# A gated short convolution moved from transposed tiles to token rows

## The chip, the cores and the metric

The kernel runs on one core of a Trainium2 chip. Its time is the device time in microseconds (us), median over the timed runs; 259.68 us before the change (three runs, 259.32 to 259.75). The engines of the core are TensorE (PE, with PEld for its weight loads), VectorE (DVE), ScalarE (ACT), GpSimd (POOL) and SyncE (SP), which here issues every transfer.

## The reference

Two layers over 256 tokens of width 1024, in float32. Layer 0 is a gated short convolution, layer 1 attention over one block of 256 keys. The part that the change touches:

```
b_gate, c_gate, xv, z = split(rms_norm(x) @ w_in, 4)     # 256 x 1024 each
u = c_gate * xv
conv[t] = w[0] * u[t-2] + w[1] * u[t-1] + w[2] * u[t]     # per channel, zero before token 0
y = b_gate * conv * silu(z)
h = x + y @ w_out
```

## The kernel before, in words

**Products.** Every dense product is done in three float32r products on PE: high part by high part, high by low, low by high. A weight unit is 256 rows by 512 columns of a matrix; there are 80 of them. A load pair brings two units (1 MB, line 314, tile `raw`, a ring of four); ACT rounds a unit into `whi` (line 355), DVE subtracts to get `wlo` (line 362), both in rings of five units; PE then runs 12 products of 512 columns (lines 419 to 421). Counting from 0, units 0 to 3 come with x in the first loads (`in_first`), and pair n (n from 2) holds units 2n and 2n+1.

**The convolution layer.** Its input projection runs in two halves of 512 channels: units 0 to 15 and 16 to 31. Each half has four blocks of four units, in the order C, x, z, B. A block fills two PSUM banks (tile `mm`), one for each 128 tokens, with tokens on the partitions and channels along the free dimension. Before the change C is scaled out of PSUM (`scaled`, line 477) and multiplied with x to u (`times`, line 485). Then PE turns u (`transposed`, line 451: eight 128x128 transposes for a half, `at<-ident,row`), so that channels lie on the partitions and tokens along the free dimension. There a shift by one or two tokens is an offset in the access, and a tap is one number for each partition: ACT scales by the last tap (line 512), DVE adds the other two (line 520). B times silu(z) is turned as well (eight more transposes), multiplied with the convolution (line 539) and split into `ys` (lines 493 and 497), the left-hand operand of the output projection, units 32 to 39. So a half has two pieces of eight transposes: u's, one unit after the x block (units 9 and 25 follow them), and y's, one unit after the B block (units 17 and 33 follow them).

**What sets the order.** All work is listed as operations with an engine, an estimated duration, what they read and write and which ring buffer they take. A planner (`Plan`) places them by these estimates, twelve times over with priorities from the round before, and keeps the best; the engines then run their instructions in that fixed order. SP's transfers are in it too: a transfer that waits holds up every later one on SP, and an operation that waits holds up all later ones of its engine.

Of the kernel before, what the change touches and what calls it, by code (L numbers as in the profile page):

```python
# [8 lines left out]
F32 = mybir.dt.float32  # L9
# [5 lines left out]
P = 128  # L15
# [15 lines left out]
)  # L31
NU = len(UNITS)
WARM = 8
NSM = 48

# [167 lines left out]
def hybrid_kernel(  # L203
    ctx: ExitStack,
    tc: tile.TileContext,
    first: bass.AP,
    xt: bass.AP,
    w: bass.AP,
    out: bass.AP,
# [40 lines left out]

    act.preload_act_table(AF.Silu)

    sm = one.tile([P, NSM], F32, name="sm")
# [8 lines left out]
    kk2 = one.tile([P, 2, 4, 2, S], F32R, name="kk2")  # L262
    kT, klz = kk2[:, :, :, 0], kk2[:, :, :, 1]
    qT = one.tile([P, 2, 4, S], F32R, name="qT")
    vv = one.tile([P, 2, 4, 4, HD], F32R, name="vv")
    g0, g1, taps = sm[:, 0:8], sm[:, 8:16], sm[:, 16:40]
# [52 lines left out]
    load_first(0, "w")  # L319
    for k in range(1, KT):  # L320
        load_first(k)
    op("DVE", 80, lambda: dve.tensor_copy(sm, piece(0, -NSM, 0)), r=[(firsts[0], (0, "x"))], w=["sm"])
# [14 lines left out]

    op("POOL", 900, lambda: make_identity(nc, ident), w=["ident"])
    op("POOL", 1000, distances, w=["dist"])
    for s in range(2):  # L340
        r2 = slice(HD - s * HD, P - s * HD)
        op("POOL", 950, lambda s=s, r2=r2: pool.memset(klz[r2, s].bitcast(F32), 0.0), w=[("klz0", s)])


    his, los = [whi_t() for _ in range(NU)], [wlo_t() for _ in range(NU)]
# [142 lines left out]
        )  # L488
        return o

    def split_y(y, j0, nj):
        js = range(j0, j0 + nj)
        op("ACT", 150 + 250 * nj, lambda: act.copy(ys[:, j0 : j0 + nj, 0], y()[:, 0:nj]), r=[y], w=[("ys", j, 0) for j in js])
        op(
            "DVE",
            180 + 280 * nj,
            lambda: dve.tensor_sub(ys[:, j0 : j0 + nj, 1], y()[:, 0:nj], ys[:, j0 : j0 + nj, 0].bitcast(F32)),
            r=[y] + [("ys", j, 0) for j in js],
            w=[("ys", j, 1) for j in js],
        )  # L500

    def conv(hf, i, us_):
        j0 = 4 * hf + 2 * i
        bank = transposed(lambda t: us_[t](), us_, [2 * i * P, (2 * i + 1) * P])
        c = bias_t()
        for jj in range(2):
            j = j0 + jj
            b = lambda jj=jj: bank()[:, jj * S : (jj + 1) * S]
            op(
                "ACT",  # L510
                440,
                lambda b=b, j=j, jj=jj: act.activation(c()[:, jj], b(), AF.Copy, scale=taps[:, 16 + j : 17 + j]),
                r=[bank, "sm"],
                w=[(c, jj)],
            )
            for d in (1, 2):
                op(
                    "DVE",
                    460,
                    lambda b=b, j=j, jj=jj, d=d: dve.scalar_tensor_tensor(  # L520
                        c()[:, jj, d:S],
                        b()[:, 0 : S - d],
                        taps[:, 8 * (2 - d) + j : 8 * (2 - d) + j + 1],
                        c()[:, jj, d:S],
                        op0=ALU.mult,
                        op1=ALU.add,
                    ),
                    r=[bank, "sm"],
                    w=[(c, jj)],
                )  # L530
        return c

    def gated(hf, i, c, qs):
        bank = transposed(lambda t: qs[t](), qs, [2 * i * P, (2 * i + 1) * P])
        y = y_t()
        op(
            "DVE",
            700,
            lambda: dve.tensor_mul(y(), c(), bank().rearrange("p (j s) -> p j s", s=S)),
            r=[(c, 0), (c, 1), bank],  # L540
            w=[y],
        )
        split_y(y, 4 * hf + 2 * i, 2)

    for hf in range(2):
        banks = block(xs, "xs")
        if hf == 0:
            stats0()
        cs = [scaled(banks[t], t) for t in range(2)]
        banks = block(xs, "xs")  # L550
        us_ = [times(banks[t], t, cs[t]) for t in range(2)]
        convs = [conv(hf, i, us_) for i in range(2)]
        banks = block(xs, "xs")
        sl = [scaled(banks[t], t, AF.Silu) for t in range(2)]
        banks = block(xs, "xs")
        qs = [times(banks[t], t, sl[t]) for t in range(2)]
        for i in range(2):
            gated(hf, i, convs[i], qs)


    for cb in range(2):
# [50 lines left out]

    def small_ones():
        dve.tensor_scalar(epsv, v1, EPS, None, op0=ALU.mult)
        dve.tensor_mul(gg, sm[:, 40:41], sm[:, 41:42])
# [11 lines left out]
    def queries_or_keys(name, bank, t):  # L627
        sq, ss, n = row_t(), ss_t(), row_t()
        op("ACT", 620, lambda: act.activation(sq(), bank(), AF.Square), r=[bank], w=[sq])

        op("DVE", 680, lambda: dve.tensor_reduce(ss()[:, 0:8], sq().rearrange("p (h d) -> p h d", d=HD), axis=AX.X, op=ALU.add), r=[sq], w=[ss])

        def inverse():
            pool.tensor_scalar(ss()[:, 0:8], ss()[:, 0:8], 1.0 / HD, epsv[:, t : t + 1], op0=ALU.mult, op1=ALU.add)
            pool.tensor_tensor(ss()[:, 8:16], ss()[:, 0:8], nhalf, op=ALU.pow)  # L635

        op("POOL", 1900, inverse, r=["nhalf", "epsv"], w=[ss])
        op(
            "DVE",
            700,  # L640
            lambda: dve.tensor_mul(
                n().rearrange("p (h d) -> p h d", d=HD),
                bank().rearrange("p (h d) -> p h d", d=HD),
                ss()[:, 8:16, None].to_broadcast([P, 8, HD]),
            ),
            r=[bank, ss],
            w=[n],
        )
        tb = at_t()

        def turn():
            for i in range(4):
                pe.transpose(tb()[:, i * P : (i + 1) * P], n()[:, i * P : (i + 1) * P], ident)  # L653

        op("PE", 440, turn, r=[n, "ident"], w=[tb])
        ts = slice(t * P, (t + 1) * P)
        psv = lambda: tb().rearrange("p (j t) -> p j t", t=P)
        for s in range(2):
            r, r2 = slice(s * HD, s * HD + HD), slice(HD - s * HD, P - s * HD)
            if name == "k":  # L660
                hi = kT[r, s, :, ts]
                op("ACT", 680, lambda r=r, hi=hi: act.activation(hi, psv()[r], AF.Copy, scale=gg[r]), r=[tb, "gg"], w=[("k", t, s, 0)])
                op(
                    "DVE",
                    745,
                    lambda r=r, s=s, hi=hi: dve.scalar_tensor_tensor(
                        klz[r, s, :, ts], psv()[r], gg[r], hi.bitcast(F32), op0=ALU.mult, op1=ALU.subtract
                    ),
                    r=[tb, "gg", ("k", t, s, 0)],
                    w=[("kl", t, s)],  # L670
                )
                op("POOL", 640, lambda r2=r2, s=s, hi=hi: pool.tensor_copy(kT[r2, s, :, ts], hi.bitcast(F32)), r=[("k", t, s, 0)], w=[("k", t, s, 1)])
            else:
                hi = qT[r, s, :, ts]
                op("ACT", 600, lambda r=r, hi=hi: act.copy(hi, psv()[r]), r=[tb], w=[("q", t, s, 0)])
                op(
                    "DVE",
                    690,
                    lambda r=r, r2=r2, s=s, hi=hi: dve.tensor_sub(qT[r2, s, :, ts], psv()[r], hi.bitcast(F32)),
                    r=[tb, ("q", t, s, 0)],  # L680
                    w=[("q", t, s, 1)],
                )

    def values(bank, t):
# [31 lines left out]
    def pair(j, s2):  # L716
# [6 lines left out]

        def scores():
            for s in range(2):
                a, b, o = qT[:, s, jj, 0:P], qT[:, s, jj, P:S], sc[s]()
                o1 = o[:, 0:S].rearrange("p (i k) -> p i k", k=P)
                pe.matmul(o1, lhsT=a, rhs=kk2[:, s, jj, :, 0:P], start=True, stop=True)
                pe.matmul(o[:, S:512], lhsT=b, rhs=kT[:, s, jj], start=True, stop=False)  # L729
                pe.matmul(o[:, S:512], lhsT=b, rhs=klz[:, s, jj], start=False, stop=True)  # L730

        op(
            "PE",
            710,
            scores,
            r=[(n, t, s, i) for n in "kq" for t in range(2) for s in range(2) for i in range(2)]
            + [("kl", t, s) for t in range(2) for s in range(2)]
            + [("klz0", s) for s in range(2)],
            w=sc,
        )  # L740
        cut = ((slice(0, P), slice(P, S)), (slice(P, 384), slice(0, S)))
# [194 lines left out]
```

## Time and profile before

| | |
|---|---|
| timed runs, median | 259.68 us (259.32 to 259.75) |
| the profiled execution, its own time | 259.06 us |
| its span | 257.3 us |
| busy: PE / DVE / ACT / POOL | 98% / 73% / 63% / 19% |
| bytes moved by the DMA engines | 45.33 MB, 176 GB/s over the span |

Times within the program are counted from the start of the span. Instructions on PE overlap, so the distance between two starts tells more than the duration of one. A mean duration can mix shapes; where it matters a stretch of the timeline is read instead.

### The profile page before, as it was taken

The page shows a single profiled execution, that of the slowest core. Times are in us where ns is not written, and L with a number is a line of the kernel's source. Part 1 is how long each engine was busy: PE and PEld are TensorE (multiplying, and loading weights), DVE is VectorE, ACT ScalarE, POOL GpSimd, SP SyncE. Part 2 cuts the span into 40 slices and gives each one's busy share as a digit, 9 for nine tenths or more (in the row PEclk, how much of TensorE's full clock was granted, in tenths as well). Part 3 has the DMA queues.
Part 4 walks back from the last instruction along what each step waited for, and adds up shares of the span by engine and source line. Part 5 has one row for each costly group of instructions (what it writes and reads, how often), then busy time and mean ns, then how long its engine had stood idle before and what let it go on. Part 6 is the DMA issues. An engine that isn't in the chain of part 4 may idle for free.

```text
span 257.3 us, 3436 instructions
## 1 busy us (share of the span) xinstructions
PE 251.8 (98%) x1198; PEld 206.8 (80%) x1198; DVE 188.7 (73%) x335; ACT 163.3 (63%) x286; POOL 49.7 (19%) x76
## 2 busy tenths in 40 slices
PE   8999999999999999999999999999999999999994
PEld 3688888888888888888888888888888888888873
DVE  2874985575558458667767976984999899977973
ACT  4868655345445535474557668996887777988720
POOL 5001000000000000000636511242164901045230
PEclk9999999999999999999999999999999999999999
DMA  6999985554666444654655454053094504400004
GB/s 216 398 395 416 383 318 164 167 171 161 225 223 201 163 163 163 176 190 173 227 169 211 138 191 163 3 169 157 3 284 152 219 3 164 164 0 3 0 0 163
DMA packets 12657, 45.33 MB, mean 176 GB/s; under 512 B 864, under 2 KB 1248, under 8 KB 12640
## 3 DMA queue, kind: packets, MB, share of 16 engines
q1 hardware_dynamic: 12640, 45.12, 49.6%
q8 instruction: 9, 0.15, 0.2%
q14 instruction: 8, 0.07, 0.1%
HBM read 44.06 MB, written 1.05 MB: 175 GB/s over the span
## 4 chain that ended last, share of the span: by engine, by line
PE 87%; DVE 4%; ACT 3%; DMA 2%; issue 1%; POOLq 0%; SPq 0%; POOL 0%
PE mm L421 26%; PE mm L419 26%; PE mm L420 26%; DMA raw<-in_first_dram 2%; PE at L451 2%; PE at L799 2%; PE at L653 1%; DVE wlo L362 1%; DVE y L838 1%; ACT whi L355 1%; PE at L820 1%; ACT prob L761 1%; DVE pp L806 1%; PE at L730 1%; PE at L729 1%
## 5 line engine op out<-in xcount | busy, mean ns | idle before, releaser
L362 DVE TENSOR_TENSOR wlo<-raw,whi 128x1024 fp32r<-128x1024 f32 (+1 forms) x84 | 98.0, 1175 | 43.0 <-ACT whi L355 42.7
L355 ACT CAST whi<-raw 128x1024 fp32r<-128x1024 f32 (+1 forms) x84 | 84.5, 1012 | 69.7 <-PE mm L421 56.5
L419 PE MATMUL mm<-whi,xs 128*128 128x512 f32 x252 | 100.3, 398 | 0.2 <-ACT xs L373 0.2
L421 PE MATMUL mm<-whi,xs 128*128 128x512 f32 x252 | 98.5, 391 | 0.0
L420 PE MATMUL mm<-wlo,xs 128*128 128x512 f32 x252 | 98.3, 390 | 0.0
L421 PEld LDWEIGHTS mm<-whi,xs 128*128 128x128 f32 x252 | 47.3, 188 | 10.4 <-DVE xs L380 0.2
L419 PEld LDWEIGHTS mm<-whi,xs 128*128 128x128 f32 x252 | 47.4, 188 | 9.4 <-ACT xs L373 0.6
L420 PEld LDWEIGHTS mm<-wlo,xs 128*128 128x128 f32 x252 | 47.4, 188 | 9.0
L419 PE MATMUL mm<-whi,ys 128*128 128x512 f32 (+1 forms) x64 | 25.4, 397 | 0.0
L421 PE MATMUL mm<-whi,ys 128*128 128x512 f32 (+1 forms) x64 | 24.9, 389 | 0.3 <-POOL ys L844 0.3
L420 PE MATMUL mm<-wlo,ys 128*128 128x512 f32 (+1 forms) x64 | 24.7, 386 | 0.0
L459 POOL TENSOR_TENSOR stat<-stat,nhalf 128x2 f32<-128x2 f32 x2 | 1.4, 709 | 118.1 <-DVE stat L458 118.1
L838 DVE TENSOR_TENSOR y<-at,y 64x256 f32<-64x256 f32 x32 | 13.5, 421 | 4.6 <-ACT y L836 3.8
L721 POOL TENSOR_SCALAR bias<-dist 128x256 f32<-128x256 f32 x16 | 9.1, 569 | 30.5 <-DVE sums L751 28.5
L761 ACT ACTIVATE prob<-neg,sums 128x256 f32<-128x256 f32 (+1 forms) x32 | 14.3, 449 | 1.0 <-DVE sums L751 0.9
L421 PEld LDWEIGHTS mm<-whi,ys 128*128 128x128 f32 x64 | 12.0, 188 | 3.2 <-POOL ys L844 0.7
L420 PEld LDWEIGHTS mm<-wlo,ys 128*128 128x128 f32 x64 | 12.1, 188 | 2.1
L419 PEld LDWEIGHTS mm<-whi,ys 128*128 128x128 f32 x64 | 12.0, 188 | 2.0
L635 POOL TENSOR_TENSOR ss<-ss,nhalf 128x8 f32<-128x8 f32 x8 | 13.1, 1641 | 0.7
L844 POOL TENSOR_TENSOR ys<-y,ys 128x256 fp32r<-128x256 f32 x8 | 7.7, 962 | 18.1 <-ACT ys L840 18.1
L775 POOL TENSOR_TENSOR sg<-row,sums 128x128 f32<-128x128 f32 x16 | 7.1, 463 | 16.9 <-ACT row L711 10.6
L802 ACT CAST pp<-at 128x384 fp32r<-128x384 f32 x16 | 7.5, 480 | 2.0 <-PE at L799 1.9
(95 smaller groups left out, 260.8 us busy)
## 6 DMA issues: line engine op xcount, KB each, us to landing
raw<-in_w_dram SPq DMA_DIRECT2D x38, 1024.0 KB, 4.9
raw<-in_first_dram SPq DMA_DIRECT2D x7, 384.0 KB, 6.5
h<-in_x_dram SPq DMA_DIRECT2D x2, 512.0 KB, 8.2
out_dram<-row SPq DMA_DIRECT2D x3, 256.0 KB, 2.5
raw<-in_first_dram SPq DMA_DIRECT2D x1, 256.0 KB, 2.7
out_dram<-row SPq DMA_DIRECT2D x2, 128.0 KB, 2.2
raw<-in_first_dram SPq DMA_DIRECT2D x1, 152.0 KB, 2.6
```

The lines of the kernel that those rows point to most:

```text
L355: lambda c=c, src=src: act.copy(his[u]()[:, c], src()),
L362: lambda c=c, src=src: dve.tensor_sub(los[u]()[:, c], src(), his[u]()[:, c].bitcast(F32)),
L419: pe.matmul(o, lhsT=a, rhs=wh, start=(k == first_k), stop=False)
L420: pe.matmul(o, lhsT=a, rhs=wl, start=False, stop=False)
L421: pe.matmul(o, lhsT=b, rhs=wh, start=False, stop=(k == KT - 1))
L635: pool.tensor_tensor(ss()[:, 8:16], ss()[:, 0:8], nhalf, op=ALU.pow)
L721: op("POOL", 450, lambda s=s, slope=slope: pool.tensor_scalar(b()[:, s], dist, slope, 1.0, op0=ALU.mult, op1=ALU.mult), r=["dist", "epsv"] ...
L761: lambda s=s, c=c, i=i, neg=neg: act.activation(p[s]()[:, c], neg()[:, c], AF.Exp, bias=sums()[:, i : i + 1], scale=-1.0, accum_out=sums() ...
L775: lambda t=t: pool.tensor_mul(sg()[:, t].rearrange("p (s d) -> p s d", d=HD), s2[t]()[:, jj * P : (jj + 1) * P].rearrange("p (s d) -> p s ...
L802: op("ACT", 480, lambda s=s, tb=tb: act.copy(pp()[:, s, 0], tb()[:, 0:384]), r=[tb], w=[(pp, (s, 0))])
L838: op("DVE", 430, lambda s=s, r=r, c=c: dve.tensor_add(y()[r, 1], av[s]()[r, c], y()[r, 1]), r=[av[s]], w=[(y, s)])
L844: lambda: pool.tensor_sub(ys[:, j, 1], y()[:, 0], ys[:, j, 0].bitcast(F32)),
```

## The change: tokens stay on the partitions

u is no longer turned. With tokens on the partitions a shift by d tokens moves rows to other partitions, so SP issues transfers within the chip: rows 0 to 127-d of u (both token halves) go to rows d to 127 of a second tile, and the last d rows of the first token half go to the head of the second. The taps, one number for each channel, now vary along the free dimension; a copy for every partition is loaded (12 KB for each partition, 1.57 MB, line 334 of the changed kernel). DVE multiplies the shifted and unshifted u by the taps and adds (five operations of 128x1024), multiplies silu(z) with the result (two of 128x512) and that with B; only this y is turned. The tiles for taps, u and shifted u share their memory with the keys and queries of the attention layer, which come later; zeroing the unused half of the keys' low parts moves behind the convolution.

```diff
-NSM = 48
+NSM = 32
...
+    kk_t = ring("kk", 1, [P, 4096], F32R, one)
+    qq_t = ring("qq", 1, [P, 2048], F32R, one)
+    early, shifted, kkb, qqb = kk_t(), qq_t(), kk_t(), qq_t()
...
     load_pair(2)
+    op("SP", us(P * 12288), lambda: sp.dma_start(early()[:, 0:3072].bitcast(F32), taps_b), w=[(early, "taps")])
...
-    def conv(hf, i, us_):
-        j0 = 4 * hf + 2 * i
-        bank = transposed(lambda t: us_[t](), us_, [2 * i * P, (2 * i + 1) * P])
-        c = bias_t()
...
+    def conv(hf, banks, cs):
+        for d in (1, 2):
+            op("POOL", 300, lambda d=d: pool.memset(u_before(d)[0:d, 0], 0.0), w=[(shifted, (d, "zero"))])
+        for t in range(2):
+            op(
+                "DVE",
+                740,
+                lambda t=t: dve.scalar_tensor_tensor(
+                    u_at(t), banks[t](), r0[:, t : t + 1], cs[t](), op0=ALU.mult, op1=ALU.mult
+                ),
+                r=[banks[t], cs[t], "r0"],
+                w=[(early, ("u", t))],
+            )
+        for d in (1, 2):
+            op(
+                "SP",
+                1400,
+                lambda d=d: sp.dma_start(u_before(d)[d:P], u_both()[0 : P - d]),
+                r=[(early, ("u", t)) for t in range(2)],
+                w=[(shifted, (d, "main"))],
+            )
+            op(
+                "SP",
+                480,
+                lambda d=d: sp.dma_start(u_before(d)[0:d, 1], u_at(0)[P - d : P]),
+                r=[(early, ("u", 0))],
+                w=[(shifted, (d, "head"))],
+            )
+        tb = lambda k: tapsb(hf, k)[:, None, :].to_broadcast([P, 2, 512])
...
+                lambda d=d: dve.tensor_mul(u_before(d), u_before(d), tb(2 - d)),
...
+        op("DVE", 1230, lambda: dve.tensor_mul(u_both(), u_both(), tb(2)), r=[(early, "taps")], w=[(early, ("u", t)) for t in range(2)])
...
+            lambda: dve.tensor_add(u_before(1), u_before(1), u_before(2)),
...
+            lambda: dve.tensor_add(u_before(1), u_before(1), u_both()),
...
+    def gated(hf, sl):
...
+                lambda t=t: dve.tensor_mul(sl[t](), sl[t](), u_before(1)[:, t]),
...
+    def output(hf, i, ys_):
+        bank = transposed(lambda t: ys_[t](), ys_, [2 * i * P, (2 * i + 1) * P])
...
+        op("ACT", 620, lambda: act.copy(ys[:, j0 : j0 + 2, 0], ps()), r=[bank], w=[("ys", j, 0) for j in js])
...
-        us_ = [times(banks[t], t, cs[t]) for t in range(2)]
-        convs = [conv(hf, i, us_) for i in range(2)]
+        conv(hf, banks, cs)
         banks = block(xs, "xs")
         sl = [scaled(banks[t], t, AF.Silu) for t in range(2)]
+        gated(hf, sl)
         banks = block(xs, "xs")
-        qs = [times(banks[t], t, sl[t]) for t in range(2)]
+        ys_ = [times(banks[t], t, sl[t]) for t in range(2)]
```

How the orders differ at three places. First SP, from the middle of the first half's loads on; before, only weight loads stand there (`raw`), each waiting for a free buffer:

```order
L314 DMA raw<-in_w_dram 128x2x1024 [waits DMAHW5_49,DVE_49]
L314 DMA raw<-in_w_dram 128x2x1024 [waits DMAHW6_49,DVE_49]
L314 DMA raw<-in_w_dram 128x2x1024 [waits DMAHW7_49,DMAHW3_49,DVE_49]
L314 DMA raw<-in_w_dram 128x2x1024 [waits DMAHW4_49,DMAHW0_49,DVE_49]
L314 DMA raw<-in_w_dram 128x2x1024 [waits DMAHW1_49,DVE_49]
```

After, the first of these rows is pair 8's load, `kk` is the tile that holds the taps and u, `qq` the one that holds the shifted u:

```order
L324 DMA raw<-in_w_dram 128x2x1024 [waits DMAHW5_49,DVE_49]
L334 DMA kk<-in_taps_dram 128x3072
L517 DMA qq<-kk 127x1024 [waits DMAHW3_49,DVE_49]
L524 DMA qq<-kk 1x16x32 [waits DMAHW4_49]
L517 DMA qq<-kk 126x1024
L524 DMA qq<-kk 2x512 [waits DMAHW6_49]
L324 DMA raw<-in_w_dram 128x2x1024 [waits DMAHW7_49,Activation_49]
L324 DMA raw<-in_w_dram 128x2x1024 [waits DMAHW0_49,DVE_49]
```

The taps and the four transfers of u stand between pair 8's load and pair 9's.

Second DVE, first half. Before, behind the product that makes u (line 485), tap products (line 520) between weight splits (line 362):

```order
L485 SCALAR_TENSOR_TENSOR row<-mm,stat,row 128x512 [waits PE_49,Pool_49]
L485 SCALAR_TENSOR_TENSOR row<-mm,stat,row 128x512 [waits PE_49]
L362 TENSOR_TENSOR wlo<-raw,whi 128x1024 [waits Activation_49]
L362 TENSOR_TENSOR wlo<-raw,whi 128x1024 [waits DMAHW7_49,Activation_49]
L362 TENSOR_TENSOR wlo<-raw,whi 128x1024 [waits Activation_49]
L520 SCALAR_TENSOR_TENSOR bias<-at,sm,bias 128x255 [waits PE_49,Activation_49]
```

After, from the split of unit 12 to the products that make y; the two rows with line 534 are the tap products of the shifted u:

```order
L370 TENSOR_TENSOR wlo<-raw,whi 128x1024 [waits DMAHW7_49,Activation_49]
L507 SCALAR_TENSOR_TENSOR kk<-mm,stat,row 128x512 [waits Pool_49]
L507 SCALAR_TENSOR_TENSOR kk<-mm,stat,row 128x512 [waits PE_49]
...
L370 TENSOR_TENSOR wlo<-raw,whi 128x1024 [waits DMAHW1_49,Activation_49]
L534 TENSOR_TENSOR qq<-qq,kk 128x1024 [waits DMAHW4_49,DMAHW3_49,DMAHW2_49]
L534 TENSOR_TENSOR qq<-qq,kk 128x1024 [waits DMAHW6_49,DMAHW5_49]
L538 TENSOR_TENSOR kk<-kk 128x1024 [waits DVE_49]
L542 TENSOR_TENSOR qq<-qq 128x1024 [waits DVE_49]
L549 TENSOR_TENSOR qq<-qq,kk 128x1024 [waits DVE_49]
L370 TENSOR_TENSOR wlo<-raw,whi 128x1024 [waits Activation_49]
L559 TENSOR_TENSOR row<-row,qq 128x512 [waits DVE_49]
L493 SCALAR_TENSOR_TENSOR row<-mm,stat,row 128x512 [waits DVE_49,PE_49] x2
```

The split ahead of line 534 is unit 16's, the one behind line 549 unit 17's; the five operations of the convolution stand in one block between them, and the first two wait for transfers.

Third DVE, second half, after the change, from the products that make u:

```order
L507 SCALAR_TENSOR_TENSOR kk<-mm,stat,row 128x512 [waits PE_49] x2
L370 TENSOR_TENSOR wlo<-raw,whi 128x1024 [waits DMAHW4_49,Activation_49]
L370 TENSOR_TENSOR wlo<-raw,whi 128x1024 [waits Activation_49]
L534 TENSOR_TENSOR qq<-qq,kk 128x1024 [waits DMAHW1_49,DMAHW0_49,Pool_49]
L370 TENSOR_TENSOR wlo<-raw,whi 128x1024 [waits DMAHW5_49,Activation_49]
L534 TENSOR_TENSOR qq<-qq,kk 128x1024 [waits DMAHW3_49,DMAHW2_49]
L370 TENSOR_TENSOR wlo<-raw,whi 128x1024 [waits Activation_49]
L538 TENSOR_TENSOR kk<-kk 128x1024 [waits DVE_49]
L370 TENSOR_TENSOR wlo<-raw,whi 128x1024 [waits DMAHW6_49,Activation_49]
L542 TENSOR_TENSOR qq<-qq 128x1024 [waits DVE_49]
L549 TENSOR_TENSOR qq<-qq,kk 128x1024 [waits DVE_49]
```

Here the splits of units 28 and 29 stand ahead of the first tap product, those of units 30, 31 and 32 behind the first, the second and the third; units 33 to 35 follow behind the gates. On PE the eight transposes of u are gone from each half, and those of y stand where the gate's stood, between units 16 and 17 and between units 32 and 33.

## Rows read from the trace of the kernel before

**Rows 1.** The page: busy time by engine, and the chain that ended last.

```profile
PE 251.8 (98%) x1198; PEld 206.8 (80%) x1198; DVE 188.7 (73%) x335; ACT 163.3 (63%) x286; POOL 49.7 (19%) x76
...
PE 87%; DVE 4%; ACT 3%; DMA 2%; issue 1%; POOLq 0%; SPq 0%; POOL 0%
```

**Rows 2.** Waits of PE: line, releaser, us in total, times, longest.

```profile
PE at L273 <- DVE nhalf L330: 1.2, 1, 1.2
PE mm L421 <- POOL ys L844: 0.3, 1, 0.3
```

**Rows 3.** The chain in order of time, 50 to 101 us: start, us, what.

```profile
53.80 0.87 PE at L451 x8
...
76.48 0.87 PE at L451 x8
...
99.17 0.87 PE at L451 x8
```

**Rows 4.** Timeline of PE around the first transposes: start, us, instruction.

```profile
30.95 1.04 PE L451 MATMUL at<-ident,row 128*128 128x128 f32 x8
31.74 0.47 PE L419 MATMUL mm<-whi,xs 128*128 128x512 f32 x1
32.05 0.39 PE L420 MATMUL mm<-wlo,xs 128*128 128x512 f32 x1
```

**Rows 5.** Timeline of PE, 0 to 16 us; the last two are 20 products apart.

```profile
1.17 3.60 PE L273 MATMUL at<-zero 128*128 128x512 bf16 x8 [1.17 <-DVE nhalf L330]
4.57 1.96 PE L405 MATMUL mm<-whi,xs 128*128 128x512 f32 x4
...
11.22 0.39 PE L419 MATMUL mm<-whi,xs 128*128 128x512 f32 x1
...
15.75 0.39 PE L421 MATMUL mm<-whi,xs 128*128 128x512 f32 x1
```

**Rows 6.** Groups by line: instruction, count, busy us, mean ns, idle before.

```profile
L520 DVE SCALAR_TENSOR_TENSOR bias<-at,sm,bias 128x255 f32<-128x255 f32 (+1 forms) x16 | 6.7, 473 | 0.0
...
L512 ACT ACTIVATE bias<-at,sm 128x256 f32<-128x256 f32 x8 | 3.1, 473 | 0.0
...
L539 DVE TENSOR_TENSOR y<-bias,at 128x512 f32<-128x512 f32 x4 | 2.7, 684 | 1.7 <-PE at L451 1.7
```

**Rows 7.** Timeline of DVE, 26 to 47 us.

```profile
27.96 1.40 DVE L485 SCALAR_TENSOR_TENSOR row<-mm,stat,row 128x512 f32<-128x512 f32 x2
29.28 2.35 DVE L362 TENSOR_TENSOR wlo<-raw,whi 128x1024 fp32r<-128x1024 f32 x2
...
41.31 1.23 DVE L362 TENSOR_TENSOR wlo<-raw,whi 128x1024 fp32r<-128x1024 f32 x1 [1.10 <-ACT whi L355]
...
46.76 1.22 DVE L362 TENSOR_TENSOR wlo<-raw,whi 128x1024 fp32r<-128x1024 f32 x1 [1.50 <-ACT whi L355]
```

**Rows 8.** Timeline of DVE, 86 to 104 us.

```profile
101.99 1.28 DVE L497 TENSOR_TENSOR ys<-y,ys 128x512 fp32r<-128x512 f32 x2
```

**Rows 9.** Stretches of PE: PE busy, granted clock, DMA share, GB/s.

```profile
10.00:12.00 2.00, 2.00 (x10) 1.00 1.04 419
26.00:28.00 2.00, 2.00 (x11) 1.00 1.03 422
```

**Rows 10.** Timeline of SP, 24 to 34 us: issues of load pairs 8 to 10.

```profile
26.93 6.92 SPq L314 DMA_DIRECT2D raw<-in_w_dram  x3
```

**Rows 11.** The page: DMA packets, and the queue that SP issues to.

```profile
DMA packets 12657, 45.33 MB, mean 176 GB/s; under 512 B 864, under 2 KB 1248, under 8 KB 12640
...
q1 hardware_dynamic: 12640, 45.12, 49.6%
```

**Rows 12.** The page: DMA issues, count, KB each, median us from issue to landing.

```profile
raw<-in_w_dram SPq DMA_DIRECT2D x38, 1024.0 KB, 4.9
...
raw<-in_first_dram SPq DMA_DIRECT2D x1, 152.0 KB, 2.6
```

More of the change, by code (lines that the diff above doesn't have):

```diff
@@ L251, in hybrid_kernel @@
     act.preload_act_table(AF.Silu)
-    sm = one.tile([P, NSM], F32, name="sm")
+    sm = one.tile([P, 48], F32, name="sm")
     ident = one.tile([P, P], F32, name="ident")
@@ L489, in times @@
         return o
-    def split_y(y, j0, nj):
-        js = range(j0, j0 + nj)
-        op("ACT", 150 + 250 * nj, lambda: act.copy(ys[:, j0 : j0 + nj, 0], y()[:, 0:nj]), r=[y], w=[("ys", j, 0) for j in js])
+    def conv(hf, banks, cs):
[27 more added lines that the diff above has]
+        tb = lambda k: tapsb(hf, k)[:, None, :].to_broadcast([P, 2, 512])
+        parts = ("zero", "main", "head")
+        for d in (1, 2):
+            op(
+                "DVE",
+                1230,
+                lambda d=d: dve.tensor_mul(u_before(d), u_before(d), tb(2 - d)),
+                r=[(early, "taps")],
+                w=[(shifted, (d, p)) for p in parts],
+            )
+        op("DVE", 1230, lambda: dve.tensor_mul(u_both(), u_both(), tb(2)), r=[(early, "taps")], w=[(early, ("u", t)) for t in range(2)])
@@ L494, in split_y @@
         op(
             "DVE",
[L496 to L499, printed above, removed]
-        )
-    def conv(hf, i, us_):
-        j0 = 4 * hf + 2 * i
-        bank = transposed(lambda t: us_[t](), us_, [2 * i * P, (2 * i + 1) * P])
-        c = bias_t()
[L506 to L531, printed above, removed]
@@ L533, in gated @@
-    def gated(hf, i, c, qs):
-        bank = transposed(lambda t: qs[t](), qs, [2 * i * P, (2 * i + 1) * P])
-        y = y_t()
+            1230,
+            lambda: dve.tensor_add(u_before(1), u_before(1), u_before(2)),
+            r=[(shifted, (2, p)) for p in parts],
+            w=[(shifted, (1, p)) for p in parts],
+        )
+        op(
+            "DVE",
+            1230,
+            lambda: dve.tensor_add(u_before(1), u_before(1), u_both()),
+            r=[(early, ("u", t)) for t in range(2)],
+            w=[(shifted, (1, p)) for p in parts] + ["convolved"],
+        )
@@ new lines, in gated @@
+    def gated(hf, sl):
+        for t in range(2):
+            op(
+                "DVE",
+                700,
+                lambda t=t: dve.tensor_mul(sl[t](), sl[t](), u_before(1)[:, t]),
+                r=[(shifted, (1, p)) for p in ("zero", "main", "head")],
+                w=[sl[t]],
+            )
+    def output(hf, i, ys_):
+        bank = transposed(lambda t: ys_[t](), ys_, [2 * i * P, (2 * i + 1) * P])
+        j0 = 4 * hf + 2 * i
+        ps = lambda: bank().rearrange("p (j s) -> p j s", s=S)
+        js = (j0, j0 + 1)
+        op("ACT", 620, lambda: act.copy(ys[:, j0 : j0 + 2, 0], ps()), r=[bank], w=[("ys", j, 0) for j in js])
@@ L538, in gated @@
             700,
-            lambda: dve.tensor_mul(y(), c(), bank().rearrange("p (j s) -> p j s", s=S)),
-            r=[(c, 0), (c, 1), bank],
-            w=[y],
+            lambda: dve.tensor_sub(ys[:, j0 : j0 + 2, 1], ps(), ys[:, j0 : j0 + 2, 0].bitcast(F32)),
+            r=[bank] + [("ys", j, 0) for j in js],
+            w=[("ys", j, 1) for j in js],
         )
-        split_y(y, 4 * hf + 2 * i, 2)
     for hf in range(2):
@@ L550, in hybrid_kernel @@
         banks = block(xs, "xs")
-        us_ = [times(banks[t], t, cs[t]) for t in range(2)]
-        convs = [conv(hf, i, us_) for i in range(2)]
+        conv(hf, banks, cs)
         banks = block(xs, "xs")
         sl = [scaled(banks[t], t, AF.Silu) for t in range(2)]
+        gated(hf, sl)
         banks = block(xs, "xs")
-        qs = [times(banks[t], t, sl[t]) for t in range(2)]
+        ys_ = [times(banks[t], t, sl[t]) for t in range(2)]
         for i in range(2):
-            gated(hf, i, convs[i], qs)
+            output(hf, i, ys_)
+    for s in range(2):
+        r2 = slice(HD - s * HD, P - s * HD)
+        op("POOL", 950, lambda s=s, r2=r2: pool.memset(klz()[r2, s].bitcast(F32), 0.0), r=["convolved"], w=[(kkb, ("klz0", s))])
     for cb in range(2):
@@ L919 @@
     dup = lambda a: np.concatenate([np.asarray(a), np.asarray(a)]).reshape(P, 1)
-    first = [cols(norm_g[0]), cols(norm_g[1])] + [cols(conv_w[0][i]) for i in range(3)]
-    first += [dup(q_norm_g[0]), dup(k_norm_g[0]), np.zeros((P, NSM - 42), np.float32)]
+    first = [cols(norm_g[0]), cols(norm_g[1])]
+    first += [dup(q_norm_g[0]), dup(k_norm_g[0]), np.zeros((P, NSM - 18), np.float32)]
     first += [b for k in range(KT) for b in (xT[k], pieces[k // 2][:, 512 * (k % 2) : 512 * (k % 2) + 512])]
```

57 lines of the change are left out of this document (30 added, 27 removed).

## The prediction

> **What bounds the kernel now.** I read the page first: TensorE (PE) is busy 98% of the span and makes up 87% of the chain that ended last [rows 1]. Then the waits of PE: the reader is to see that after the start it waited once, for 0.3 us [rows 2]. So the span is the sum of PE's products and transposes, and anything that takes an instruction off PE shortens it, as long as nothing that PE waits for comes late. Third, the chain in order of time around the convolution [rows 3]: eight transposes (line 451) stand in one piece of 0.87 us at 53.80, 76.48 and 99.17, and a fourth such piece begins at 30.95 [rows 4].
>
> **The price of a piece of transposes.** Products run 0.2265 us apart (20 steps from 11.22 to 15.75 [rows 5]), so a unit of 12 products takes 2.72 us. From 53.80 to 76.48 lie 22.68 us, which is 8 units (21.75 us) and one piece: 0.93 us. That is more than the 0.87 us of the chain because the product behind the transposes starts late (31.74 to 32.05, 0.31 instead of 0.23 [rows 4]). The change takes out two of the four pieces, those of u: **-1.86 us** on PE.
>
> **Other work that goes or comes, off the path.** DVE loses 16 tap products (6.7 us) and 4 products with a PSUM operand (2.7 us), ACT loses 8 scalings (3.1 us) [rows 6]. DVE gains ten operations on 128x1024 and four on 128x512. The first are like the weight splits, 1.15 us when back to back (two in 2.35 us [rows 7]); the second I price by the two subtractions in 1.28 us [rows 8], 0.65 us each. That makes 14.1 us against 9.4 us: 4.7 us more DVE work over 90 us in which DVE idles a third of the time; alone it costs nothing. The two memsets of klz move on POOL behind the convolution, long before keys are written. The 1.57 MB of taps take 3.75 us at 419 GB/s [rows 9] and stand in SP's queue before load pair 9 (units 18 and 19); it was issued about 30.5 (the second of three issues that begin at 26.93 [rows 10]), unit 18 was split at 46.76 [rows 7] and multiplied at 57.4 (one unit and one piece after 53.80), so 3.75 us are covered by the 10 us or so between the median landing and that split. The end of the attention part is re-ordered a little; I give that 0.3 us either way and no sign.
>
> **The step that decides: the shift by transfer.** In the changed kernel's order SP issues for each half a transfer of 127 rows of 4 KB, one of 126 rows, and two small heads, and DVE multiplies the shifted u in the very next steps. No transfer in this trace goes from SBUF to SBUF and none has 127 rows. What the rows show is how a transfer is dealt out: there are 864 packets under 512 B, which is 16 for each of the 54 transfers (38+7+2+3+1+2+1 in the seven lines of the list of issues, of which the first and the last stand here), so every transfer ends on 16 engines, and all of them have 128 rows or twice that, 8 or 16 for each engine [rows 11, 12]. The order shows the same from the other side: the one-row head was cut by the program's builder into 16 pieces of 32, the 127 rows were not cut. If the shares have to be equal, 127, being prime, has only one share.
> - Low bound: dealt like the others, 0.52 MB at 419 GB/s, 1.3 us.
> - High bound: one engine alone. An engine moves 419/16/1.04 = 25.2 bytes per ns in a full stretch [rows 9], and 45.12 MB in 49.6% of 16 x 257.3 us = 22.1 over the whole program [rows 11]. 127 x 4096 = 520,192 bytes then take 20.6 to 23.5 us.
> I take the high bound at its lower figure, 20.6 us, since the other engines stand still meanwhile, and since every row has equal shares. The 126 rows have equal shares of 9 on 14 engines: 9 x 4096/25.2 = 1.5 us.
>
> The Trainium skill has a rule for this (DMA: Bandwidth & Descriptors, "Why a DMA increments its semaphore by 16 and not by 1"): a transfer from the sync queue runs on the largest number of engines up to 16 that divides its slowest dimension, and 127 partitions go to a single engine. No run here shows it with 127 rows; by it the sum is the one that follows, and without it the first rival's.
>
> **The sum, first half.** Times are in the clock of before. PE would reach the transposes of y at 53.80 - 0.93 = 52.87. u is formed once unit 12 is split: the two products that ran at 27.96 now stand behind that split (29.28 plus 2.35 [rows 7]) and end near 32. Pair 8's load, issued at 26.93 [rows 10] into full queues (422 GB/s, [rows 9]), needs its median 4.9 us [rows 12] to about 32; the taps follow to 35.8. Then one engine carries the shift: 35.8 + 20.6 = 56.4, and its share of the 126 rows to 57.9. DVE waits there with unit 17's split queued behind: second tap product from 58.0, four operations of 1.15 to 62.6, the split to 63.8, two gate products to 65.1, two products with the bank (0.7 each [rows 7]) to 66.5, 0.2 to PE: 66.7. PE stands still for **13.8 us**.
> At the start, after idling, eight products of 512 columns ran from 1.17 to 4.57, 0.43 us apart, and later ones 0.23 [rows 5]: the lower of the clock's two levels, 1.2 instead of 2.4 GHz. With the four that follow the spell is 3.4 to 5.4 us long, and half of it is lost. I charge **2 us** for one such spell after this stall (nothing to 2.7 as ends).
>
> **Second half.** PE is now 15.8 us late. Unit 24 starts at 76.48 - 2.72 - 0.93 + 15.8 = 88.6; u is ready near 90.2; a load pair was issued just before, so the engine is free between 91.3 and 93.3, say 92.2; the shift lands at 112.8. Here the order puts the split of unit 30 behind the first tap product: 112.8 + 2 x 1.15 = 115.1, PE at 115.3. It would have been there at 76.48 + 0.93 + 5 x 2.72 - 1.86 + 15.8 = 104.9: **10.4 us** of stall. DVE then has six operations of 1.15 (122.0), two gates (123.3), three splits (126.8), two products (128.2): transposes at 128.4. PE, three units on, would be there at 123.5: another **4.9 us**, in which any slow clock after the second stall disappears. 128.4 against 99.17 is **29.2 us late** for good (13.8 + 2 + 10.4 + 4.9 - 1.86), since from there PE feeds everything and does not wait. The profiled execution took 259.06 us, 1.8 more than its span; 259.06 + 29.2 = 288.3. The median of the timed runs lies 0.6 above the profiled one, so 288.9, rounded to **289 us**.
>
> **Rivals.**
> - *The shift is dealt over all engines.* It lands at 37.1 and 38.4, before DVE gets to the tap products: unit 16's split, at 41.31 in before [rows 7], comes first, at 40.4. Five operations from 41.6 to 47.4, a split to 48.5, gates to 49.8; the last bank of the half is done at 53.80 - 2.72 - 0.93 = 50.15, y is formed by 51.8 and PE gets there at 52.87. No stall: 259.68 - 1.86 = **257.8 us**, faster. For it: every transfer here uses 16 engines. Against it: none has a row count without a divisor. It decides from a shift of about 2.5 us each; above that PE waits.
> - *The shift is dealt over a few engines, say four, 5.2 us each.* The two transfers land at 41.0 and 46.2, the second tap product slips 3.5 us, and about 2 us of it reach PE in the first half (it has 1.1 to 1.5 us of slack). In the second half they land near 82.6 and 87.8, three operations and splits later than in the first rival; y comes 1.5 us late. 257.8 + 3.6 = **261.4 us**, slightly slower.
> - *The extra 1.57 MB of taps starve the weights* (the change costs, but not by the shift). Against it speaks the cover of 10 us named above; its price would be at most those 3.75 us: 261.6. I give it nothing of its own.
>
> **How the numbers follow.** One engine: 0.80. All engines: 0.13. A few engines or late taps: 0.07, of which 0.03 end near no change. The likeliest case's own range: an engine 15% faster than in these rows takes 6 us off and no slow clock 2 more, the start of the second shift is open by 1 to 2 us, which makes 278; 23.5 us for a shift adds 5.8 and a slow clock after the second stall up to 2.4, and with the same start 299. The range that I give for all is 270 to 305, which leaves out mainly the first rival. Changes below 0.2% (0.5 us) can't be told from none here. Faster 0.13, same 0.03, slower 0.84.
>
> **What would show it.** Right: a PE gap of about 14 us ahead of the transposes of y at 53 us, with DVE waiting for the transfer of 127 rows; a second of about 10 us in the last block of the second half, ahead of a product that waits for a split (wlo), and a third of 3 to 5 us at the second transposes; a mean DMA share near a sixteenth in those stretches; landing about 20 us after the transfer is taken up, loads behind it late as well. The two transpose pieces of u gone. Wrong: landing of the shift within 3 us of its turn, no DMA wait on DVE, and a span shorter by about 1.9 us; or PE gaps that end on something else, such as a load of weights.

## The result and the profile after

The changed kernel takes **297.74 us** (median of 4 runs, 296.16 to 298.24) against 259.5 us for the kernel before on the same chip: ratio 1.146, 95% interval 1.142 to 1.151. It is slower by 38 us, and nearly all of it is visible as time in which PE stands still or runs at the lower clock. The profiled execution took 298.24 us, its span 296.4 us.

The page after; the PE, PEclk and DMA rows are tenths in 40 slices of 7.4 us, the last two rows are the chain that ended last, by engine and by line:

```profile
PE 257.3 (87%) x1182; PEld 208.9 (70%) x1182; DVE 194.7 (66%) x329; ACT 160.2 (54%) x278; POOL 53.2 (18%) x80
...
PE   8999999105999970587999999999999999999995
...
PEclk9999999855999995597999999999999999999999
DMA  6999818604756061049363564541706551700003
...
PE 58%; DMA 17%; DVE 12%; SPq 4%; ACT 4%; issue 3%; POOL 1%; POOLq 0%; DVEq 0%
PE mm L429 17%; PE mm L427 17%; PE mm L428 17%; DMA qq<-kk 15%; DVE wlo L370 4%; SPq L524 3%; ACT whi L363 2%; DMA raw<-in_first_dram 2%; PE at L459 2%; DVE y L875 1%; PE at L836 1%; PE at L690 1%; DVE kk L507 1%; DVE qq L534 1%; DVE qq L549 1%
```

PE was 98% busy and 87% of the chain [rows 1]; now it is 87% and 58%, and the transfers of u (`qq<-kk`) are 15% of the chain. Two holes stand out in the PE row (a third is shorter than a slice), and in or just before each the DMA row falls to 0 or 1 tenth: the engine that carries the rows is one of sixteen. Within each of the two PEclk falls to 5: the granted clock is 0.5 from 57.5 to 74.6 us and from 112.1 to 125.8, and once more from 136.0 to 139.4, behind the third hole.

The waits of PE (us in total, times, longest); before there was one of 0.3 us after the start [rows 2]:

```profile
PE at L459 <- DVE row L493: 19.5, 3, 16.6
PE mm L428 <- DVE wlo L370: 13.1, 1, 13.1
...
PE mm L429 <- POOL ys L881: 0.5, 1, 0.5
PE at L857 <- DVE pp L843: 0.5, 1, 0.5
PE mm L427 <- ACT ys L877: 0.2, 1, 0.2
```

What these releasers wait for in turn, on DVE:

```profile
DVE qq L534 <- DMA qq<-kk: 40.8, 2, 22.2
```

DVE's timeline in the first half (start, duration, operation, idle time before it and what ended it) shows the queue behind that wait: the tap products, the split of unit 17 and the gates all stand behind one instruction.

```profile
60.74 2.57 DVE L534 TENSOR_TENSOR qq<-qq,kk 128x1024 f32<-128x1024 f32 x2 [18.64 <-DMA qq<-kk]
63.23 1.22 DVE L538 TENSOR_TENSOR kk<-kk 128x1024 f32<-128x1024 f32 x1
64.37 1.22 DVE L542 TENSOR_TENSOR qq<-qq 128x1024 f32<-128x1024 f32 x1
65.62 1.22 DVE L549 TENSOR_TENSOR qq<-qq,kk 128x1024 f32<-128x1024 f32 x1
66.76 1.22 DVE L370 TENSOR_TENSOR wlo<-raw,whi 128x1024 fp32r<-128x1024 f32 x1
67.89 1.29 DVE L559 TENSOR_TENSOR row<-row,qq 128x512 f32<-128x512 f32 x2
69.10 1.40 DVE L493 SCALAR_TENSOR_TENSOR row<-mm,stat,row 128x512 f32<-128x512 f32 x2
```

PE's timeline around the end of the first hole; it shows the transposes of y at 69.99, 17 us behind the last product ahead of them (52.96), and products 0.43 us apart behind them, at the granted clock of 0.5, the lower of the two levels (1.2 GHz):

```profile
52.96 0.39 PE L429 MATMUL mm<-whi,xs 128*128 128x512 f32 x1
69.99 2.32 PE L459 MATMUL at<-ident,row 128*128 128x128 f32 x8 [16.65 <-DVE row L493]
71.97 0.78 PE L427 MATMUL mm<-whi,xs 128*128 128x512 f32 x1
72.54 0.63 PE L428 MATMUL mm<-wlo,xs 128*128 128x512 f32 x1
72.97 0.63 PE L429 MATMUL mm<-whi,xs 128*128 128x512 f32 x1
```

Windows of the same trace (length, busy PE, granted clock, DMA share of 16 engines, GB/s):

```profile
36.00:42.00 6.00, 6.00 (x28) 1.00 0.07 29
45.00:56.00 11.00, 8.34 (x37) 1.00 0.94 294
57.00:60.00 3.00, 0.00 (x0) 0.58 0.07 27
60.00:70.00 10.00, 0.01 (x1) 0.50 0.17 44
...
112.00:122.00 10.00, 0.00 (x0) 0.51 0.07 27
```

A share of 0.07 at 27 to 29 GB/s is one engine at its full rate: before, a full stretch had 16 engines at 419 GB/s, 26 each [rows 9]. Between 45 and 56 us the other engines move the weight loads that are queued behind.

SP's timeline shows a price that I had not seen: the one-row head behind the transfer of 127 rows takes 9 us to issue, and the 126 rows and the loads start that much later.

```profile
32.56 0.76 SPq L517 DMA_DIRECT2D qq<-kk  x1
33.38 9.05 SPq L524 DMA_DIRECT2D qq<-kk  x1
42.48 0.87 SPq L517 DMA_DIRECT2D qq<-kk  x1
43.40 0.64 SPq L524 DMA_DIRECT2D qq<-kk  x1
44.14 24.24 SPq L324 DMA_DIRECT2D raw<-in_w_dram  x4
...
93.48 0.63 SPq L517 DMA_DIRECT2D qq<-kk  x1
94.16 9.76 SPq L524 DMA_DIRECT2D qq<-kk  x1
103.96 0.84 SPq L517 DMA_DIRECT2D qq<-kk  x1
```

**Where the time went, by place.** PE's products come in the same order, twelve for each unit, so the start of a unit's first product minus that of the kernel before says how late PE is there. I worked this out from the two traces for each kernel with a changed convolution (us, from one profiled execution each):

| start of unit | 4 | 16 | 18 | 30 | 31 | 34 | 75 | 79 |
|---|---|---|---|---|---|---|---|---|
| the change | +0.48 | -0.44 | +18.75 | +17.82 | +32.90 | +37.73 | +37.50 | +39.42 |
| 127 rows in the second half only | +0.95 | +0.03 | +0.02 | -0.91 | +14.06 | +17.00 | +16.43 | +17.77 |
| 112 and 15 rows | +0.86 | -0.02 | -0.03 | -0.96 | -0.96 | -0.96 | -1.44 | +0.08 |
| no shift | +0.91 | +0.03 | +0.02 | -0.91 | -0.91 | -0.94 | -1.16 | +0.77 |
| 126 and 1 rows | +0.46 | -0.46 | -0.48 | -1.41 | -1.41 | -1.45 | -1.51 | -1.38 |
| 126 and 1, first transfer of 304 columns | -0.19 | -1.11 | -1.13 | -2.06 | -2.06 | -2.09 | -2.09 | -1.97 |

Read along the first line: 0.92 gained with the first piece of transposes (unit 4 to 16), 19.2 lost at the first hole, 0.93 gained with the second piece, 15.1 and 4.8 lost at the second and third holes, 1.9 lost in the last five units (1.7 net from unit 34 to 79). In between, products of the attention part stand between the units, in an order that differs from kernel to kernel, so the attention part is best read from unit 34 to unit 79 as a whole.

### The profile page after: what moved, and what is told of

The parts are those of the page before. It is cut to its first block, busy times and chain, and to the rows that moved or that the text cites. A ratio compares the mean times of both kernels' runs of the same rounds, so it can differ in the third digit from the quotient of the medians.

```text
span 296.4 us, 3420 instructions
## 1 busy us (share of the span) xinstructions
PE 257.3 (87%) x1182; PEld 208.9 (70%) x1182; DVE 194.7 (66%) x329; ACT 160.2 (54%) x278; POOL 53.2 (18%) x80
## 4 chain that ended last, share of the span: by engine, by line
PE 58%; DMA 17%; DVE 12%; SPq 4%; ACT 4%; issue 3%; POOL 1%; POOLq 0%; DVEq 0%
PE mm L429 17%; PE mm L427 17%; PE mm L428 17%; DMA qq<-kk 15%; DVE wlo L370 4%; SPq L524 3%; ACT whi L363 2%; DMA raw<-in_first_dram 2%; PE at L459 2%; DVE y L875 1%; PE at L836 1%; PE at L690 1%; DVE kk L507 1%; DVE qq L534 1%; DVE qq L549 1%
## 5 line engine op out<-in xcount | busy, mean ns | idle before, releaser
L363 ACT CAST whi<-raw 128x1024 fp32r<-128x1024 f32 (+1 forms) x84 | 84.1, 1011 | 105.5 <-PE mm L429 57.5
L428 PE MATMUL mm<-wlo,xs 128*128 128x512 f32 x252 | 99.6, 395 | 13.1 <-DVE wlo L370 13.1
L428 PEld LDWEIGHTS mm<-wlo,xs 128*128 128x128 f32 x252 | 48.1, 191 | 22.9 <-DVE wlo L370 13.5
L429 PEld LDWEIGHTS mm<-whi,xs 128*128 128x128 f32 x252 | 48.0, 191 | 10.5 <-DVE xs L388 0.2
L427 PEld LDWEIGHTS mm<-whi,xs 128*128 128x128 f32 x252 | 48.2, 191 | 9.2
L534 DVE TENSOR_TENSOR qq<-qq,kk 128x1024 f32<-128x1024 f32 x4 | 4.9, 1223 | 40.9 <-DMA qq<-kk 40.8
L427 PE MATMUL mm<-whi,ys 128*128 128x512 f32 (+1 forms) x64 | 26.1, 408 | 0.2 <-ACT ys L877 0.2
L429 PE MATMUL mm<-whi,ys 128*128 128x512 f32 (+1 forms) x64 | 25.5, 398 | 0.5 <-POOL ys L881 0.5
L459 PE MATMUL at<-ident,row 128*128 128x128 f32 x16 | 3.6, 363 | 19.6 <-DVE row L493 19.5
L459 PEld LDWEIGHTS at<-ident,row 128*128 128x128 f32 x16 | 2.4, 179 | 20.9 <-POOL qq L502 17.0
L429 PEld LDWEIGHTS mm<-whi,ys 128*128 128x128 f32 x64 | 12.4, 194 | 3.8 <-POOL ys L881 1.3
L427 PEld LDWEIGHTS mm<-whi,ys 128*128 128x128 f32 x64 | 12.4, 193 | 2.8 <-ACT ys L877 0.6
L595 POOL MEMSET kk<- 64x1024 f32 x2 | 1.9, 952 | 60.1 <-DMA raw<-in_w_dram 60.0
```

Source lines behind the costliest of these rows:

```text
L363: lambda c=c, src=src: act.copy(his[u]()[:, c], src()),
L427: pe.matmul(o, lhsT=a, rhs=wh, start=(k == first_k), stop=False)
L428: pe.matmul(o, lhsT=a, rhs=wl, start=False, stop=False)
L429: pe.matmul(o, lhsT=b, rhs=wh, start=False, stop=(k == KT - 1))
L459: pe.transpose(bank()[:, (2 * i + t) * P : (2 * i + t + 1) * P], src(t)[:, c : c + P], ident)
L534: lambda d=d: dve.tensor_mul(u_before(d), u_before(d), tb(2 - d)),
```

## The experiments

The theory: a transfer of 127 rows is carried by one engine, each half's DVE work waits for it, and nothing else in the change costs more than a microsecond or two. The rivals: the DVE work and the taps cost as well; the shift costs by being a transfer within the chip, whatever its rows.

**112 rows and 15.** Both shifts are cut so that their large part has a share for every engine:

```diff
-                lambda d=d: sp.dma_start(u_before(d)[d:P], u_both()[0 : P - d]),
...
+            for part, a, b in {1: (("main", 0, 112), ("rest", 112, 127)), 2: (("main", 0, 112), ("rest", 112, 126))}[d]:
...
+                    lambda d=d, a=a, b=b: sp.dma_start(u_before(d)[a + d : b + d], u_both()[a:b]),
```

> The shift by d rows is cut into a transfer of 112 rows and one of the remaining 15 or 14, nothing else. Theory (127 rows are carried by one DMA engine, row by row, and the stalls are DVE waiting for that): the shift lands 2 to 4 us after its turn, both PE gaps of 17.0 and 13.5 us go, and so does the half clock behind them; 257.8 to 260 us, the upper end if the re-ordered end of the attention part keeps the 1.7 us that it costs now. Rival A (a copy from SBUF to SBUF is slow whatever its row count): 290 to 298 us as before the cut. Rival B (the change has other costs on DVE or by the taps' load that the stalls hide): in between, 262 to 275 us, with PE waiting for DVE that waits for no transfer.

Measured: 259.0 us (258.34 to 259.49), ratio 0.9994 (0.998 to 1.0005). All three holes are gone, and DVE's longest wait for these transfers is

```profile
DVE qq L535 <- DMA qq<-kk: 1.0, 1, 1.0
```

So the 38 us hang on how the rows are dealt out. But the 1.86 us of transposes do not come out in the time. The table says where they go: 0.9 us at the start (unit 4, where PE waits for ACT's first rounding of x), and 1.0 us from unit 34 to 79 (-0.96 to +0.08), in the attention part, where the planner has chosen another order and PE waits 0.9 us for POOL:

```profile
PE mm L413 <- ACT xs L381: 1.4, 1, 1.4
...
PE mm L429 <- POOL ys L882: 0.9, 2, 0.5
```

**126 rows and the last one.** The 126 rows have shares of 9 on 14 engines:

```diff
-                lambda d=d: sp.dma_start(u_before(d)[d:P], u_both()[0 : P - d]),
...
+            for part, a, b in {1: (("main", 0, 126), ("rest", 126, 127)), 2: (("main", 0, 126),)}[d]:
...
+                    lambda d=d, a=a, b=b: sp.dma_start(u_before(d)[a + d : b + d], u_both()[a:b]),
```

> The transfer of 127 rows is cut into one of 126 rows and one of the last row; the transfers for the shift by two stay at 126 rows. Theory (equal shares: 126 rows go to 14 engines, 9 each): lands as fast as with 112 rows, the time within 1% of the 112-row kernel, 257.8 to 260.5 us. If only multiples of 16 rows are spread and 126 rows also go to one engine: two serial transfers of 20 us each half, 310 us or more. Rival A (copies within the chip are slow): 290 to 298 us.

Measured: **257.56 us** (257.38 to 257.86), ratio 0.9942 (0.993 to 0.996): 0.6% faster than before, a small gain but clear of the noise. The first rival's price in the prediction was 257.8 us. 14 engines do as well as 16, and one row more or less in a transfer is worth 40 us. Against the version of 112 rows, the planner's order of the attention part is a kinder one: 0.1 us is lost from unit 34 to 79. The traces show why: from unit 34 on, PE's 750 instructions stand here in the very order of the kernel before, while with 112 rows 84 places differ from it and in the changed kernel 49. DVE's wait for the transfers:

```profile
DVE qq L535 <- DMA qq<-kk: 1.5, 1, 1.5
```

**No shift at all.** The tap products read the unshifted u and the four transfers of each half are gone; the shift by one and two tokens is left out of the computation.

```diff
-                lambda d=d: sp.dma_start(u_before(d)[d:P], u_both()[0 : P - d]),
...
-                lambda d=d: sp.dma_start(u_before(d)[0:d, 1], u_at(0)[P - d : P]),
...
-                lambda d=d: dve.tensor_mul(u_before(d), u_before(d), tb(2 - d)),
...
+                lambda d=d: dve.tensor_mul(u_before(d), u_both(), tb(2 - d)),
```

> No transfer of u at all: the tap products read the unshifted u, so the shift by one and two tokens is left out of the computation; taps, DVE operations and the order of PE stay. Theory: the same time as the 112-row kernel within 0.5%, since a shift that lands in 3 us is hidden; 257.8 to 260 us, PE ahead of before by 0.93 us after unit 9 and 1.86 us after unit 25. Rival B (other costs on DVE or by the taps): above 262 us here too.

Measured: 259.35 us (258.59 to 259.77), ratio 1.0004 (0.999 to 1.002). With no transfer PE is where it is with 112 rows up to unit 70, to within 0.1 us: a shift that is dealt out costs nothing. From unit 34 on, PE's 750 instructions stand in exactly the order of the changed kernel here, and 1.7 us go from unit 34 to 79 (-0.94 to +0.77), as they do there: that is the price of the new order of the attention part, which I had put at 0.3 without a sign. The waits that the profile names there make 1.2 of it:

```profile
PE mm L429 <- POOL ys L866: 0.5, 1, 0.5
PE at L842 <- DVE pp L828: 0.5, 1, 0.5
PE mm L427 <- ACT ys L862: 0.2, 1, 0.2
```

**Row counts by themselves.** The kernel before, with four transfers between rows of `xs` that nothing reads any more, behind the last weight load, each waiting for the one ahead: 112, 126, 124 and 127 rows of 4 KB.

> The kernel before, and behind its last weight load four transfers of 4 KB rows from SBUF to SBUF, of 112, 126, 124 and 127 rows one after another, each waiting for the one before; nothing uses what they move, the stretch has no other transfers until the output. Theory, at 159 ns a row on each engine and about 1.9 us of fixed time: 112 rows on 16 engines 3.0 us, 126 on 14 engines 3.3, 124 on 4 engines 6.8, 127 on one engine 22 us from issue to landing. Rival A (copies within the chip are slow): all four alike, about 20 us. A ceiling of 16 equal shares with a shorter last one: 127 rows land in 3.2 us.

Measured, from issue to landing: 112 rows 3.7 us, 126 rows 3.9 us, 124 rows 10.0 us, 127 rows 22.7 us. A microsecond inside each of the four, two of the 124 rows (the last two columns are the DMA share and GB/s):

```profile
224.00:225.00 1.00, 1.00 0.93 270
228.00:229.00 1.00, 1.00 0.84 295
231.00:232.00 1.00, 1.00 0.25 61
236.00:237.00 1.00, 1.00 0.24 90
245.00:246.00 1.00, 1.00 0.06 25
```

The shares are 16, 14, 4 and 1 engines of 16: the largest number up to 16 that divides the rows. The page says it a second time, without any rate. The prediction had read one packet under 512 B for each engine of a transfer; here there are 899, 35 more than the 864 of before [rows 11], and 16 + 14 + 4 + 1 make 35:

```profile
DMA packets 13181, 47.33 MB, mean 178 GB/s; under 512 B 899, under 2 KB 1283, under 8 KB 13164
```

The four engines of the 124 rows move only 15 GB/s each at first and 23 later (single rows take up to 0.76 us there instead of 0.16), so that they took 10.0 us from issue to landing where 31 rows at the one engine's rate and the same 2 us around them would make 7; why is open. For the rival "a few engines" I had 5.2 us.

The Trainium skill's rule (DMA: Bandwidth & Descriptors, "Why a DMA increments its semaphore by 16 and not by 1"), that a transfer from a hardware queue runs on the largest number of engines up to 16 that divides its slowest dimension, agrees with all four shares.

**One half only.** 126 rows and one in the first half, 127 rows at once in the second:

```diff
-                lambda d=d: sp.dma_start(u_before(d)[d:P], u_both()[0 : P - d]),
...
+            for part, a, b in {1: (("main", 0, 126 + hf), ("rest", 126, 127))[: 2 - hf], 2: (("main", 0, 126),)}[d]:
...
+                    lambda d=d, a=a, b=b: sp.dma_start(u_before(d)[a + d : b + d], u_both()[a:b]),
```

> The split of the shift (126 rows and the last row) in the first half only; the second half keeps its one transfer of 127 rows. Theory (each shift on one engine stalls PE by itself, independent of the other): in the changed kernel PE's position went from 18.75 us late at unit 24 to 37.73 at unit 34, with the split in both halves from -0.48 to -1.45, so one half costs 18.98 + 0.97 = 20 us on top of 257.6: 277.5 us (276 to 280, the upper end where the planner orders the attention part as badly as in the changed kernel, 1.7 us). Unit 17 does not wait, units 30 and 33 do, for about 13 and 3 us. Rival (the second pair of stalls was made longer by the loads and the slow clock that the first one left behind): clearly less, 265 to 273 us.

Measured: 276.63 us (276.17 to 280.04), ratio 1.069 (1.063 to 1.076). The stalls add up, half by half. PE's waits are the second and third of the changed kernel, and the first is gone:

```profile
PE mm L428 <- DVE wlo L370: 12.7, 1, 12.7
PE at L459 <- DVE row L493: 2.5, 2, 2.2
```

In the table PE loses 17.9 us from unit 30 to 34 here and 19.9 in the changed kernel; of the 2 us between them 1.6 are the slow clock behind the third hole (36.17 at unit 33 to 37.73 at unit 34), which doesn't occur here, behind a third hole of 2.2 us instead of 2.5.

**A load beside the shift.** In the changed kernel the shift of the first half lands 24.7 us after its first row moves (35.76 to 60.43), and that of the second 26 us after its issue (93.48 to 119.45); alone 127 rows took 22.7 from the issue. To see whether the loads queued behind take the difference: three transfers at the end of the kernel before, 127 rows alone, 127 rows with a 1 MB load issued right behind, 112 rows.

> The kernel before, with three transfers within the chip behind the last weight load, each waiting for the one ahead: 127 rows of 4 KB alone, 127 rows again with one load of 1 MB issued right behind it, 112 rows. Nothing reads what they move. Theory (an engine takes turns between the transfers that wait on it, so that the load's sixteenth, 65,536 bytes, 2.6 us at 25.2 bytes per ns, comes out of the shift's time): the first lands about 22.7 us after its issue, the second about 25.3 us after. Rival (the load's share waits behind all 127 rows on that engine): both 22.7 us, and the load lands only after the shift. If the theory holds, the 25 us of the changed kernel's shifts are 20.6 us, 2 us of latency and one load or two.

SP's timeline:

```profile
222.47 23.23 SPq L866 DMA_DIRECT2D xs<-xs  x2
245.81 8.71 SPq L881 DMA_DIRECT2D raw<-in_w_dram  x1
268.50 0.59 SPq L866 DMA_DIRECT2D xs<-xs  x1
271.00 0.37 SPq L881 DMA_DIRECT2D raw<-in_w_dram  x1
```

The first took 22.6 us (222.47 to 245.10, where the second was issued), the second 23.4 (to 268.50). My theory of turns (25.3) fell. The 0.8 us are not the load's sixteenth of 2.6: that one moved after the shift, since the load landed at 271.0, 2.5 us behind it, though its other fifteen shares had landed by 259.5. So here the engine worked through its queue in the order of issue.

That settles where the shifts of the changed kernel start. In the second half the load issued at 92.16 landed at 97.04; its share stood ahead of the shift on that engine, and the shift's first row moved at 96.5. In the first half the first row moved at 35.76, as soon as the engine's share of the taps was through. From first row to landing 127 rows then took:

| 127 rows on one engine | us |
|---|---|
| alone (this experiment, and the row counts by themselves) | 21.2, 21.4 |
| a load beside them (this experiment) | 22.2 |
| second half of the changed kernel: 126 rows and a load beside | 22.9 |
| first half of the changed kernel: 126 rows and three loads beside | 24.7 |

The more the other engines move meanwhile, the longer it takes. In the first half the rows stand 0.155 us apart up to 44.0 and again from 57.8 on; the 60 rows between, while the other engines move the loads, take 0.23 each. That the loads slow the one engine fits all five numbers; by what they slow it isn't shown. DVE went on 0.3 us behind each landing (60.43 to 60.74 and 119.45 to 119.75); the head lands 0.2 behind the shift.

The 9 us of issue are here again (8.71), on a load this time: what SP issued right behind 127 rows for one engine was held up that long each time.

**The first transfer.** The change narrows the first transfer from 304 to 288 columns (`NSM`), and in five profiles of the narrow one PE is 0.46 to 0.95 us late at unit 4.

```diff
-NSM = 32
+NSM = 48
```

> The version with 126 rows and the last row in both halves, and the first transfer again 304 columns wide (48 small columns, 30 of them zeros) as before the change instead of 288. Order of all engines unchanged. Theory (the shorter first rows make the first loads land later, 0.46 us on PE at unit 2 in the version of 288 columns): the start is back, 257.1 us. Rival (the start differs for another cause, such as the order of the memsets or chance): 257.6 us, PE again 0.4 to 0.9 late at unit 2.

Measured: **256.98 us** (256.79 to 257.15), ratio 0.9908 (0.989 to 0.992): the fastest kernel of this study, and 2.5 us faster than before (259.44 beside it). The start is 0.65 us earlier than with 288 columns and the rest is the same, as the theory has it. But it isn't settled: in the profile of the experiment with the load beside, which has the kernel before's own start of 304 columns, PE was 0.45 us late at unit 4 too, so this place varies from one execution to the next (with the row counts by themselves, the same start, it was -0.07). The intervals of the two versions just miss each other (0.9924 and 0.9926), and they weren't timed side by side.

## Why the prediction was right

**The mechanism** stood as predicted: one engine for 127 rows, three holes on PE at the places named (before the transposes of y at unit 17, before unit 30's second product, before the second transposes at unit 33), DVE waiting for the transfer, a DMA share of a sixteenth, loads late. The sign and the range held; 289 us was 9 us short. By its terms:

| term | predicted | measured |
|---|---|---|
| two pieces of transposes | -1.86 | -0.92 and -0.93 |
| start of the kernel | 0 | +0.5 |
| first hole, with slow clock | 13.8 + 2 | 19.2 |
| second and third, with slow clock | 10.4 + 4.9 | 15.1 + 4.8 |
| order of the attention part | 0 (0.3 either way) | +1.7 |
| sum | 29.2 | 39.4 |

- *The piece of transposes.* Right to a hundredth (0.92 and 0.93 against 0.93).
- *The start of the kernel* was not in the sum. Why it is late by 0.5 isn't settled (see the first transfer above).
- *The shift on one engine* was priced by bytes alone, 20.6 us, and this is the term that was sized most wrongly. Alone it takes 21.2 from its first row to its landing. In the first half it began where the sum had it (35.76 against 35.8) and took 24.7, with the loads beside it, so it landed 4.0 us late (60.43 against 56.4). DVE's work from there to PE's transposes was 0.7 shorter than priced, and PE arrived 0.3 later (53.2 against 52.87): a hole of 16.8 us instead of 13.8.
- *The start of the second shift.* I freed the engine at 92.2, by a load "issued just before". That load was issued at 92.16 and landed at 97.04, the whole of its share went ahead, and the shift began at 96.5. It took 22.9, so it landed 6.7 us later than predicted (119.45 against 112.8). PE went on 6.9 us later (122.17 against 115.3) and had arrived 4.0 later: a hole of 13.3 us instead of 10.4.
- *The slow clock.* At 0.5 from 57.5 to 74.6, so 4.6 us of it with PE at work: 2.3 us lost, 2 charged. The charge was taken from the start of the program, where products stand 0.43 us apart [rows 5]; the profile records a granted clock of 1.00 there, so those rows show the pace and not its cause. Behind the hole the same pace comes with a granted clock of 0.5. I let the spell behind the second hole disappear in the third, as it did, and forgot the one behind the third: 1.6 us.
- *The attention part.* "0.3 us either way and no sign" was too small: from unit 34 to 79 it cost 1.7 us in the changed kernel and 1.7 without any shift (the same order of PE), 1.0 with 112 rows, 0.8 with one half split, and 0.1 with 126 rows and one, where PE's order is that of before. All have one sign; that PE had no slack there before [rows 2], so that a new order could mostly lose, is my reading of it.
- *DVE's added work and the taps* were priced at nothing, and cost nothing: with 126 rows and one DVE waits for the transfers once, for 1.5 us, and PE not at all at units 17, 30 and 33.
- *The first rival*, all engines, 257.8 us, is what the kernel does as soon as 127 rows become 126 and 1: 257.56. That it comes so close is in part luck: the start lost 0.5, and the planner happened to fall back to the order of before in the attention part; with 112 rows, equally spread, it was 259.0.

## What to carry to other kernels

The number of rows of a transfer decides how many engines carry it, so look at its divisors before its bytes: 127 rows as 126 and 1 is the difference between 15% slower and 0.6% faster. A wait on an in-order engine delays all that stands behind it, and a long hole in PE can cost a second time through the clock (2.3 us behind the first). Where a kernel's order comes out of a planner, time two or three equal versions before a gain of a microsecond is put down to the edit, since the planner's order elsewhere moves as much (0.1 to 1.7 us here).

## What the runs showed that I had not expected

- Behind 127 rows for one engine, SP's next issue is held up for 8.7 to 9.8 us (9.05, 9.76, 9.14 and 8.71 in four places), a small transfer or a load. Behind 126 rows on 14 engines the issues take 0.5 to 1.4 us. What holds the issue up isn't shown.
- The engine served its queue in the order of issue: a load's share came after the 127 rows, not between them (259.5 for the fifteen other shares, 271.0 for the last). So a load issued behind waits for the whole shift though its other fifteen shares are long done; in the changed kernel the load issued at 44.14 landed at 64.4.
- Transfers within the chip on four engines ran at 15 GB/s an engine at first, later at 23; on one engine 25; on fourteen 22 (295 GB/s at a share of 0.84), on sixteen 18 (270 at 0.93). Why four began as the slowest isn't settled.
